# The second half's output projection moved past the scan, on all eight PSUM banks, beside the making of the first MLP operands

## The chip, the cores and the metric

The kernel runs on one core of one Trainium2 chip. The metric is the device time of one execution in microseconds. The kernel before takes 2737.82 us, the median of three runs (2737.07 to 2745.41).

## The reference

One layer of a hybrid decoder on 2048 tokens of width 1024: RWKV-7 time mixing, a delta-rule scan over 12 heads of 64, side by side with a cross-attention into 256 memory tokens. Their outputs are concatenated, projected, and added to the input. A squared-ReLU MLP of width 4096 follows.

```python
h = rms_norm(x, norm_mix_g)
mix, q_mem = rwkv7_time_mix(h, rw_in, ...)          # scan over 2048 tokens
mem_out = memory_cross_attention(q_mem, k_mem, v_mem, ...)
x = x + jnp.concatenate([mix, mem_out], axis=-1) @ w_out
u = rms_norm(x, norm_ffn_g) @ w_ff1
x = x + jnp.square(jax.nn.relu(u)) @ w_ff2
```

## The kernel before, in words

The 2048 tokens are four groups of 512 (`NG`, `G`) or 16 pairs of two 64-token chunks. All large products are done in three passes: each operand is split into a rounded part and a rest (`split`, L92 on ACT, L93 on DVE), and high times high, high times low and low times high are accumulated in PSUM.

There are three stages. In the first, the input projections `project(g)` are made group by group, and `prepare`, `scan` and `post` run over the 16 pairs. `prepare` builds a pair's matrices and solves a small triangular system on DVE, `scan` carries the state, and `post` normalises and writes `mix_d[g]`. In the second, `output(g)` multiplies `mix_d[g]` and `mem_d[g]` by `w_out`, adds `x` and writes `x2_d[g]`. In the third, the MLP runs over two halves of 1024 tokens (`layer1`, `layer2`), each a Strassen-like scheme of seven products in place of eight. Its operands `B` are seven combinations of the normalised, transposed rows of `x2_d`, and `prologue(hf, banks)` makes them.

`output(g)` (L805 to L832) works on quarters of 256 output columns: eight weight tiles are loaded and split for a quarter, then 24 matmuls of 256 columns go into one half bank for each of two row tiles (`rows_mm`, L626). PSUM comes from the pool `psx` of three banks. Group 3 is called in two parts, since its pairs finish one by one; each part loads `w_out` again.

`prologue(0, (3, 4, 6))` loads 128 rows of `x2_d` at a time (L924), squares them on ACT (L926), takes the inverse root on GpSimd (L86), scales on DVE (L928), transposes eight blocks on TensorE (L933), copies to `xraw` on ACT (L936), and then splits and subtracts (L92, L93, L908). Its row buffer `xn` has two copies.

A planner orders the work: every instruction gets a rank (`tc.cur_priority`), lower goes first, and a list scheduler with a timing model turns the ranks into a fixed order for each engine. `dense(first, last, ...)` spreads the steps of a generator over ranks from pair `first` to pair `last`, three pairs behind the scan (`LAG`), 640 ranks to a pair; `CUTS` holds these bounds. So projection work fills the gaps of the scan. After the scan the stage's memory pools are closed, and the pools of the MLP are opened over the same addresses; `reuse_waits` orders new tiles behind the old ones. All loads and stores go through SP's queue. The MLP's PSUM is one pool with eight tags, `b0` to `b7`.

Of the kernel before, what the change touches and what calls it, by code (L numbers as in the profile page):

```python
# [9 lines left out]
F32 = mybir.dt.float32  # L10
F32R = mybir.dt.float32r
# [8 lines left out]
P = 128  # L20
# [29 lines left out]
PAIR_RANKS = 640  # L50
CUTS = [0, 3.17, 8.01, 11.51, 12.67, 13.54, 14.66, 15.27, 15.84]
SPAN = list(zip(CUTS, CUTS[1:]))

# [7 lines left out]
def hybrid_layer(  # L61
# [81 lines left out]
    mem_d = [dram.tile([P, 2, G], F32, name=f"mem_d{g}") for g in range(NG)]  # L143
    mix_d = [dram.tile([P, NB, G], F32, name=f"mix_d{g}") for g in range(NG)]
    x2_d = [dram.tile([G, D], F32, name=f"x2_d{g}") for g in range(NG)]

# [423 lines left out]
    gmc = gain_col(xp, g_mix[0], "gmc")  # L570
    gm = gain_col(xp, g_mem, "gm")
    muc = xp.tile([P, 20], F32, name="muc")
    nc.sync.dma_start(muc, rw_mu[0].rearrange("(b p) -> p b", p=P))
# [231 lines left out]
    def output(g, parts=(0, 1)):  # L805
# [14 lines left out]
        for qq in range(4):  # L820
            csl = slice(qq * 256, (qq + 1) * 256)
            w = weights256(w_out[0][:, csl])
            for t2 in parts:
# [8 lines left out]
                nc.sync.dma_start(x2_d[g][r0 : r0 + 256, csl].rearrange("(t p) c -> p t c", p=P), xr)  # L832


    def memory(*groups):
# [24 lines left out]
    tc.cur_priority = rank["base"] + 20 * PAIR_RANKS  # L860
# [15 lines left out]

    NCH = DFF // 256
    wq = ctx.enter_context(tc.tile_pool(name="c_w", bufs=2, reuse_waits="tile"))
    rp = ctx.enter_context(tc.tile_pool(name="c_r", bufs=16, reuse_waits="tile"))
    tp = ctx.enter_context(tc.tile_pool(name="c_t", bufs=2, reuse_waits="tile"))  # L880
    xs = ctx.enter_context(tc.tile_pool(name="c_x", bufs=1, reuse_waits="tile"))
    sp = ctx.enter_context(tc.tile_pool(name="c_s", bufs=8, reuse_waits="tile"))
    fp = ctx.enter_context(tc.tile_pool(name="c_f", bufs=FBUF, reuse_waits="tile"))
    pso = ctx.enter_context(tc.tile_pool(name="c_ps", bufs=1, space=PSUM, reuse_waits="tile"))

# [3 lines left out]
    def bank(i, shape, name):  # L889
        return pso.tile(shape, F32, tag=f"b{i}", name=name)  # L890

    def ft(name):
        return fp.tile([P, 512], F32, tag="f", name=name)
# [13 lines left out]
    def sub(o, a, b):  # L907
        nc.vector.tensor_tensor(o, a, b, op=ALU.subtract)  # L908
# [3 lines left out]
    def prologue(hf, banks):  # L912

        B = {n: [xs.tile([P, 4, G], F32R, name=f"x{n}{p}") for p in "hl"]
             for n in ("11", "22", "T1", "T3", "T2", "21", "T4")}
        if hf == 0:
            nc.sync.dma_start(gfr, g_ffn.to_broadcast([P, D]))
        nb = 0
        for i in range(4):
            tsl = slice(i * P, (i + 1) * P)  # L920
            raw = {}
            for l in range(2):
# [6 lines left out]
                for j in range(2):  # L929
                    pt = bank(banks[nb % len(banks)], [P, 4, P], "pt")  # L930
                    nb += 1
                    for k in range(4):
                        nc.tensor.transpose(pt[:, k, :], xn[:, (4 * j + k) * P : (4 * j + k + 1) * P], ident)  # L933
                    t = rp.tile([P, 512], F32, tag="r", name="xraw") if hf == 0 else ft("xraw")
# [3 lines left out]
            put = lambda n, src: split(src, B[n][0][:, :, tsl], B[n][1][:, :, tsl])  # L938
            b11, b12, b21, b22 = raw[0, 0], raw[0, 1], raw[1, 0], raw[1, 1]
            put("11", b11)  # L940
            put("22", b22)
            sub(b11, b12, b11)
            put("T1", b11)
            sub(b12, b22, b12)
            put("T3", b12)
            sub(b22, b22, b11)
            put("T2", b22)
            put("21", b21)
            sub(b21, b21, b22)
            put("T4", b21)  # L950
            yield
# [12 lines left out]
    def layer1(hf, B):  # L964
# [127 lines left out]

    tc.cur_priority = rank["base"] + 16 * PAIR_RANKS
    B = list(prologue(0, (3, 4, 6)))[-1]
    tc.cur_priority = rank["base"] + 20 * PAIR_RANKS
    layer1(0, B)
    got = []

    def aside():
# [38 lines left out]
```

## Time and profile before

| | us |
|---|---|
| median of three runs | 2737.82 |
| the profiled execution's own time | 2744.66 |
| its span | 2742.9 |
| TensorE matmul busy | 2610.6 (95%) |
| TensorE weight load busy | 2128.4 (78%) |
| DVE busy | 1811.1 (66%) |
| ACT busy | 1353.9 (49%) |
| GpSimd busy | 235.9 (9%) |
| DMA moved | 519.32 MB, 189 GB/s |

PE is TensorE's matmuls and PEld its weight loads, which overlap; SP is the engine that issues the transfers. Busy time is the union of an engine's instructions, and a matmul counts from its start to its modelled end, so pipelined matmuls overlap and their spacing is less than the mean duration shown. PEclk is the share of full clock that TensorE was granted. A few per cent of the matmul records can be missing, so counts of matmuls are slightly low.

### The profile page before, as it was taken

Reading aid. Unit: us, or ns where it says so; the run is one execution under the profiler, and the core shown is the slowest. Engines: PE = TensorE matmul, PEld = TensorE weight load, DVE = VectorE, ACT = ScalarE, POOL = GpSimd, SP = SyncE. Lnnn points to the kernel's source line nnn. Section 1 sums busy time; section 2 is a strip of 40 time slices with the busy share of each in tenths; the row PEclk is TensorE's granted clock in tenths of the full one; section 3 lists DMA queues with packets and bytes.
Section 4 is the critical chain, followed back from the end, with each engine's and each line's share of the span. In section 5 each row is a group of like instructions: output and inputs, shape, how many; then the busy total and the mean of one; then the engine's idle time right before and its main releaser. Section 6 shows DMA issues by size and latency. Waiting matters only on the chain.

```text
span 2742.9 us, 49338 instructions
## 1 busy us (share of the span) xinstructions
PE 2610.6 (95%) x17620; PEld 2128.4 (78%) x17620; DVE 1811.1 (66%) x4628; ACT 1353.9 (49%) x2925; POOL 235.9 (9%) x172
## 2 busy tenths in 40 slices
PE   6989999999999999979996999999999999999999
PEld 4767777777777777868885888878888888888887
DVE  5556657667767767877558777765866666655564
ACT  5563445445545546553346444444744454544443
POOL 2000011111111111111301000000000000000000
PEclk9999999999999998989997999999999999999999
DMA  8987555556555545355583667886775444456675
GB/s 254 292 265 207 161 172 148 165 151 178 151 155 139 146 134 141 102 140 142 172 257 102 234 232 262 282 304 195 243 260 165 143 150 146 157 193 208 209 255 165
DMA packets 468442, 519.32 MB, mean 189 GB/s; under 512 B 117538, under 2 KB 291682, under 8 KB 468196
## 3 DMA queue, kind: packets, MB, share of 16 engines
q1 hardware_dynamic: 468196, 516.18, 61.0%
q8 instruction: 138, 2.26, 0.3%
q14 instruction: 108, 0.88, 0.1%
HBM read 361.86 MB, written 154.14 MB: 188 GB/s over the span
## 4 chain that ended last, share of the span: by engine, by line
PE 64%; DVE 5%; DMA 4%; ACT 1%; issue 1%; SPq 1%; POOL 0%; DVEq 0%; ACTq 0%; POOLq 0%
PE pu L961 23%; PE py L1070 22%; PE pz L102 5%; PE pout L626 4%; DMA ws<-in_w_out_dram 1%; PE pp L390 1%; DVE zt L428 1%; PE prhs L482 1%; DVE wo L93 1%; PE psco L769 1%; PE pe L463 1%; PE pw L488 1%; PE pe L456 1%; PE pS L495 1%; DVE Zw L432 1%
## 5 line engine op out<-in xcount | busy, mean ns | idle before, releaser
L102 PE MATMUL pz<-xh,w 128*128 128x512 f32 x1408 | 483.0, 412 | 4.3 <-DVE last L678 3.0
L1070 PE MATMUL py<-wpl,hhh 128*128 128x512 f32 x896 | 349.1, 390 | 0.0
L1070 PE MATMUL py<-wph,hhl 128*128 128x512 f32 x896 | 348.4, 389 | 0.0
L1070 PE MATMUL py<-wph,hhh 128*128 128x512 f32 x896 | 343.9, 391 | 0.0
L102 PEld LDWEIGHTS pz<-xh,w 128*128 128x128 f32 x1408 | 267.6, 192 | 71.2 <-issue 6.4
L93 DVE TENSOR_TENSOR hhl<-hr,hhh 128x512 fp32r<-128x512 f32 x224 | 154.6, 690 | 218.4 <-ACT hhh L92 218.0
L92 ACT CAST hhh<-hr 128x512 fp32r<-128x512 f32 x224 | 139.1, 621 | 304.8 <-PE py L1070 281.6
L102 PE MATMUL pz<-xl,w 128*128 128x512 f32 x704 | 287.7, 409 | 0.6 <-DVE xl L93 0.6
L626 PE MATMUL pout<-wo,xh 128*128 128x256 f32 x1024 | 213.6, 302 | 12.9 <-ACT wo L92 7.3
L428 DVE TENSOR_TENSOR zt<-Ti,Zw 96x96 f32<-96x96 f32 (+20 forms) x736 | 154.2, 232 | 72.0 <-DMA Ti<-nd 50.7
L1070 PEld LDWEIGHTS py<-wph,hhl 128*128 128x128 f32 x896 | 168.2, 188 | 34.9
L1070 PEld LDWEIGHTS py<-wph,hhh 128*128 128x128 f32 x896 | 168.2, 188 | 34.6
L1070 PEld LDWEIGHTS py<-wpl,hhh 128*128 128x128 f32 x896 | 168.3, 188 | 34.5
L626 PEld LDWEIGHTS pout<-wo,xh 128*128 128x128 f32 x1024 | 171.9, 202 | 20.3 <-ACT wo L92 8.2
L102 PEld LDWEIGHTS pz<-xl,w 128*128 128x128 f32 x704 | 135.7, 193 | 30.7 <-issue 2.4
L93 DVE TENSOR_TENSOR wpl<-wr,wph 128x512 fp32r<-128x512 f32 x224 | 153.2, 684 | 4.2 <-ACT wph L92 4.2
L432 DVE TENSOR_TENSOR Zw<-Zw,zt 96x96 f32<-96x96 f32 (+20 forms) x736 | 150.3, 227 | 6.5 <-DVE zt L428 0.2
L626 PE MATMUL pout<-wo,xl 128*128 128x256 f32 x512 | 151.9, 297 | 0.2 <-DVE xl L93 0.2
L92 ACT CAST wph<-wr 128x512 fp32r<-128x512 f32 x224 | 138.1, 617 | 9.4 <-PE pu L961 7.0
L390 PE MATMUL pp<-AR,BK 64*128 64x128 f32 x768 | 104.4, 320 | 17.2 <-DVE PT L392 15.0
L390 PEld LDWEIGHTS pp<-AR,BK 64*128 64x128 f32 x768 | 85.6, 214 | 36.3 <-DVE PT L392 18.5
L392 DVE TENSOR_TENSOR PT<-pp,msk 128x384 f32<-128x384 f32 x128 | 67.9, 548 | 62.4 <-PE pp L390 62.1
(292 smaller groups left out, 5496.3 us busy)
## 6 DMA issues: line engine op xcount, KB each, us to landing
w<-w_d SPq DMA_DIRECT2D x264, 256.0 KB, 4.3
hr<-hc_d SPq DMA_DIRECT2D x224, 256.0 KB, 2.8
ws<-in_w_ff_dram SPq DMA_DIRECT2D x32, 1024.0 KB, 5.7
hc_d<-hs SPq DMA_DIRECT2D x128, 256.0 KB, 2.3
wr<-t_d SPq DMA_DIRECT2D x128, 256.0 KB, 3.2
wr<-in_w_ff_dram SPq DMA_DIRECT2D x96, 256.0 KB, 3.1
w_d<-w SPq DMA_DIRECT2D x88, 256.0 KB, 4.3
ws<-in_w_out_dram SPq DMA_DIRECT2D x80, 256.0 KB, 4.4
```

The costliest lines, as they stand in the source:

```text
L92: nc.scalar.copy(hi, src)
L93: nc.vector.tensor_tensor(lo, src, hi.bitcast(F32), op=ALU.subtract)
L102: nc.tensor.matmul(ps, a(k), b(k), start=(k == 0 and i == 0), stop=(k == nk - 1 and i == 2))
L390: nc.tensor.matmul(pps[q][:, j, :], BK[c][rs, b, :], d["AR"][rs, b, :], start=True, stop=True)
L392: nc.vector.tensor_tensor(PT[:, q * NB + 3 * hb : q * NB + 3 * hb + 3, :], pps[q], K["msk"].unsqueeze(1).to_broadcast([P, 3, 2 * C]), op=A ...
L428: nc.vector.tensor_tensor(zt[:, j0:j1, :nt], Ti[:, s, s + 1 :].unsqueeze(1).to_broadcast([96, j1 - j0, nt]), Zw[:, j0:j1, s : s + 1].to_br ...
L432: nc.vector.tensor_tensor(Zw[:, j0:j1, s + 1 :], Zw[:, j0:j1, s + 1 :], zt[:, j0:j1, :nt], op=ALU.add)
L456: nc.tensor.matmul(pe[lo, b, :], d["PT"][:32, q * NB + b, 32:C], te[:, q * NB + b, :], start=True, stop=True)
L463: nc.tensor.matmul(pe[hi, b, :], te2[:, b, :], Z[:, b, lo], start=True, stop=True)
L626: nc.tensor.matmul(po[:, t, :], a(k, t), w[k][:, b], start=(k == 0 and i == 0 and t == 0), stop=(k == KB - 1 and i == 2 and t == 1))
L961: nc.tensor.matmul(ps, a[u][:, k * P : (k + 1) * P], b[v][:, k, :], start=(first and k == 0 and i == 0), stop=(k == 3 and i == 2), skip_gr ...
L1070: nc.tensor.matmul(ps[bk], a[u][:, m * P : (m + 1) * P], b[v], start=(fresh and c == 0 and t == 0), stop=(c == NCH - 1 and t == 2), skip_g ...
```

## The change

Groups 2 and 3 are no longer projected by `output` beside the scan. `late_output` does them after it: the output columns in two halves of 512, eight banks in turn (0 to 3 for the first half, 4 to 7 for the second), four row tiles of 128 for each of the eight k blocks, 192 matmuls of 512 columns for a group. It keeps the split mixer output for both halves, loads `w_out` once for a group, and stores through GpSimd's queue. Between the k steps it advances a generator (`first`), which loads the normalised, transposed rows and makes the seven operands of the first MLP half.

Those rows come from `ffn_rows`, which is put behind `output(1)` in the same call of `dense`. It loads 128 rows of `x2_d`, normalises, transposes into `psx`, applies the gain while copying and writes `xn_d`. The prologue of the second MLP half stays as it was, but for the order of its splits.

The cuts are changed, the operand pool is split in two (`c_x0`, `c_x1`), the pools are opened in another order, and PSUM becomes eight pools of one bank. `layer1` and `layer2` swap banks by half.

```diff
-CUTS = [0, 3.17, 8.01, 11.51, 12.67, 13.54, 14.66, 15.27, 15.84]
+CUTS = [0, 3.17, 8.01, 11.51, 13.9, 15.84]
+    def ffn_rows():
+        for i in range(4):
+            for l in range(2):
+                xt = xrows("xt")
+                nc.sync.dma_start(xt, x2_d[l][i * P : (i + 1) * P, :])
+                rows_norm(xp, xt, xt, xp.tile([P, D], BF16, name="junk"))
+                for j in range(2):
+                    pt = psx.tile([P, 4, P], F32, tag="x", name="pt")
+                    for k in range(4):
+                        nc.tensor.transpose(pt[:, k, :], xt[:, (4 * j + k) * P : (4 * j + k + 1) * P], ident)
+                    rt = small([P, 4, P], "rt")
+                    for k in range(4):
+                        nc.scalar.activation(rt[:, k, :], pt[:, k, :], AF.Copy, scale=gfc[:, 4 * j + k : 4 * j + k + 1])
+                    nc.sync.dma_start(xn_d[i][j, l], rt)
+                    yield
...
-        elif p in (7, 11):
-            dense(*SPAN[p // 4 + 3], (output(p // 4), 64))
-        elif p in (13, 15):
-            dense(*SPAN[p // 2], (output(3, (p // 2 % 2,)), 32))
+        elif p == 7:
+            dense(*SPAN[4], (output(1), 64), (ffn_rows(), 16))
...
-    wq: c_w, rp: c_r, tp: c_t, xs: c_x, sp: c_s, fp: c_f, pso: c_ps (one pool)      [order of opening, in short]
+    xs: c_x0, tp: c_t, rp: c_r, xs2: c_x1, wq: c_w, sp: c_s, fp: c_f, pso: c_ps0 to c_ps7
...
+            for i in range(4):                       # first half: prologue(0, ())
+                raws.append({})
+                for j in range(2):
+                    for l in range(2):
+                        t = rp.tile([P, 512], F32, tag="r", name="xraw")
+                        raws[i][j, l] = t.rearrange("p (k t) -> p k t", k=4)
+                        nc.sync.dma_start(raws[i][j, l], xn_d[i][j, l])
+                yield
+            for n in names:
+                for i in range(4):
+                    combine(i, raws[i], n)
+                    yield
...
-            q = 4 * ((c + 1) % 2)
+            q = 4 * ((c + hf) % 2)
-        X, Y = range(4), range(4, 8)
+        X, Y = (range(4), range(4, 8)) if hf == 0 else (range(4, 8), range(4))
...
-    tc.cur_priority = rank["base"] + 16 * PAIR_RANKS
-    B = list(prologue(0, (3, 4, 6)))[-1]
+    def late_output(beside):
+        for g in (2, 3):
+            ops = []
+            for n in range(2):
+                ps = [bank(4 * n + m, [P, 512], "px") for m in range(4)]
+                csl = slice(n * 512, (n + 1) * 512)
+                for k in range(KB):
+                    if n == 0:
+                        mt = stile("mr")
+                        nc.sync.dma_start(mt, mix_d[g][:, k, :] if k < NB else mem_d[g][:, k - NB, :])
+                        hl = [fp.tile([P, 512], F32R, tag="f", name=f"mx{p}") for p in "hl"]
+                        split(mt, *hl)
+                        ops.append(hl)
+                    if k % 2 == 0:
+                        wt = wq.tile([P, 4, 512], F32R, tag="w", name="wx")
+                    wr = stile("wr")
+                    nc.sync.dma_start(wr, w_out[0][k * P : (k + 1) * P, csl])
+                    b = [wt[:, 2 * (k % 2) + i, :] for i in range(2)]
+                    split(wr, *b)
+                    for m in range(4):
+                        for i, (u, v) in enumerate(((0, 0), (0, 1), (1, 0))):
+                            nc.tensor.matmul(ps[m], ops[k][u][:, m * P : (m + 1) * P], b[v],
+                                             start=(k == 0 and i == 0), stop=(k == KB - 1 and i == 2))
+                    if k % 2 or g == 3 or n:
+                        next(beside, None)
+                for m2 in range(2):
+                    ...                              # xr: load x, add two banks, advance beside
+                    nc.gpsimd.dma_start(x2_d[g][rows, csl].rearrange("(t p) c -> p t c", p=P), xr)
+    tc.cur_priority = rank["base"] + 19 * PAIR_RANKS
+    beside = first()                                 # first() runs prologue(0, ())
+    late_output(beside)
+    for _ in beside:
+        pass
+    tc.cur_priority = max(tc.cur_priority, rank["base"] + 20 * PAIR_RANKS)
+    layer1(0, got[-1])
```

## Rows read from the trace of the kernel before

**Rows 1.** Page, chain that ended last: shares of the span by engine, then by line.

```profile
PE 64%; DVE 5%; DMA 4%; ACT 1%; issue 1%; SPq 1%; POOL 0%; DVEq 0%; ACTq 0%; POOLq 0%
...
PE pu L961 23%; PE py L1070 22%; PE pz L102 5%; PE pout L626 4%; DMA ws<-in_w_out_dram 1%; PE pp L390 1%; DVE zt L428 1%; PE prhs L482 1%; DVE wo L93 1%; PE psco L769 1%; PE pe L463 1%; PE pw L488 1%; PE pe L456 1%; PE pS L495 1%; DVE Zw L432 1%
```

**Rows 2.** By stretch: us; PE, PEld, DVE, ACT, POOL busy (count); PEclk, DMA share, GB/s.

```profile
1064.00:1343.00 279.00, 252.81 (x2891) 223.91 (x2892) 207.85 (x716) 134.03 (x358) 50.13 (x29) 0.91 0.46 128
...
1343.00:1447.00 104.00, 97.28 (x827) 94.60 (x823) 59.03 (x138) 40.57 (x107) 10.58 (x7) 0.97 0.73 231
...
1447.00:1487.00 40.00, 14.44 (x64) 11.20 (x62) 37.41 (x61) 31.66 (x58) 5.83 (x7) 0.57 0.36 112
...
1487.00:1490.00 3.00, 2.42 (x6) 1.96 (x7) 3.00 (x7) 2.51 (x6) 0.46 (x1) 0.50 0.00 0
...
1490.00:1790.00 300.00, 300.00 (x1281) 241.74 (x1280) 224.74 (x357) 140.63 (x242) 2.21 (x1) 0.99 0.71 244
...
1790.00:1798.00 8.00, 5.42 (x24) 4.09 (x23) 4.56 (x7) 5.42 (x10) 0.00 (x0) 0.95 0.95 341
...
2500.00:2740.00 240.00, 239.00 (x1055) 197.59 (x1053) 130.95 (x206) 96.64 (x170) 0.00 (x0) 1.00 0.65 208
```

**Rows 3.** Chain by time, 1310 to 1500 us: start us, us, what.

```profile
1348.49 0.85 PE py L525 x24
...
1429.34 17.43 PE pout L626 x143
...
1448.23 4.33 DMA xn<-x_d
...
1459.84 3.54 DMA xn<-x_d
...
1469.70 3.46 DMA xn<-x_d
...
1487.58 12.48 PE pu L961 x41
```

**Rows 4.** Lines L928, L933, 1330 to 1480: ns min/median/max, first and last start.

```profile
L928 DVE SCALAR_TENSOR_TENSOR xn<-xn,nr,gfr x8: 1276/1282/1286, 1350.5 to 1479.6; 128x1024 f32<-128x1024 f32 x8
...
L933 PE MATMUL pt<-ident,xn x56: 270/421/447, 1446.6 to 1478.4; 128*128 128x128 f32 x56
```

**Rows 5.** Adds by time on DVE; landing of stores L832, 1300 to 1330.

```profile
1313.08 0.69 DVE L831 TENSOR_TENSOR xr<-xr,pout 128x512 f32<-128x512 f32 x1 [1.16 <-PE pout L626]
...
1323.20 0.67 DVE L831 TENSOR_TENSOR xr<-xr,pout 128x512 f32<-128x512 f32 x1
...
DMA to landing us min/median/max: 2.5/2.5/2.5
```

**Rows 6.** Lines L495 and L560, 1300 to 1400: first and last start.

```profile
L495 PE MATMUL pS<-WV,BKT x48: 221/222/270, 1323.4 to 1343.1; 128*64 128x64 f32 x48
...
L560 PE MATMUL pg<-SG,g2s x24: 273/275/422, 1329.3 to 1380.1; 128*128 128x128 f32 x24
```

**Rows 7.** Groups in 2500 to 2740, then L908, L556 and landing of L971.

```profile
L93 DVE TENSOR_TENSOR hhl<-hr,hhh 128x512 fp32r<-128x512 f32 x85 | 58.7, 691 | 100.4 <-ACT hhh L92 100.4
...
L92 ACT CAST hhh<-hr 128x512 fp32r<-128x512 f32 x85 | 52.8, 621 | 134.0 <-PE py L1070 131.2 <-DMA hr<-hc_d 2.8
...
L908 DVE TENSOR_TENSOR xraw<-xraw x16: 677/683/691, 1452.9 to 1493.4; 128x512 f32<-128x512 f32 x16
...
L556 ACT ACTIVATE mixT<-pty,lbc x30: 342/367/377, 1065.9 to 1336.1; 128x128 f32<-128x128 f32 x30
...
DMA to landing us min/median/max: 5.3/7.9/10.5
```

**Rows 8.** DMA in 1343 to 1447: total, and w_out loads with us to landing.

```profile
DMA packets 26069, 24.04 MB, mean 231 GB/s; under 512 B 1376, under 2 KB 25696, under 8 KB 26058
...
ws<-in_w_out_dram SPq DMA_DIRECT2D x40, 256.0 KB, 3.6
```

**Rows 9.** Group in 1343 to 1447: busy, mean ns, idle before and its releasers.

```profile
L92 ACT CAST wo<-ws 128x256 fp32r<-128x256 f32 x87 | 32.0, 404 | 46.9 <-DMA ws<-in_w_out_dram 31.2 <-PE pout L626 14.3 <-DVE wo L93 0.7
```

More of the change, by code (lines that the diff above doesn't have):

```diff
@@ L144, in hybrid_layer @@
     mix_d = [dram.tile([P, NB, G], F32, name=f"mix_d{g}") for g in range(NG)]
+    xn_d = [dram.tile([2, 2, P, 4, P], F32, name=f"xn_d{i}") for i in range(4)]
     x2_d = [dram.tile([G, D], F32, name=f"x2_d{g}") for g in range(NG)]
@@ L571, in hybrid_layer @@
     gm = gain_col(xp, g_mem, "gm")
+    gfc = gain_col(xp, g_ffn[0], "gfc")
     muc = xp.tile([P, 20], F32, name="muc")
@@ L877, in hybrid_layer @@
     NCH = DFF // 256
+    xs = ctx.enter_context(tc.tile_pool(name="c_x0", bufs=1, reuse_waits="tile"))
+    tp = ctx.enter_context(tc.tile_pool(name="c_t", bufs=2, reuse_waits="tile"))
+    rp = ctx.enter_context(tc.tile_pool(name="c_r", bufs=16, reuse_waits="tile"))
+    xs2 = ctx.enter_context(tc.tile_pool(name="c_x1", bufs=1, reuse_waits="tile"))
     wq = ctx.enter_context(tc.tile_pool(name="c_w", bufs=2, reuse_waits="tile"))
-    rp = ctx.enter_context(tc.tile_pool(name="c_r", bufs=16, reuse_waits="tile"))
-    tp = ctx.enter_context(tc.tile_pool(name="c_t", bufs=2, reuse_waits="tile"))
-    xs = ctx.enter_context(tc.tile_pool(name="c_x", bufs=1, reuse_waits="tile"))
     sp = ctx.enter_context(tc.tile_pool(name="c_s", bufs=8, reuse_waits="tile"))
     fp = ctx.enter_context(tc.tile_pool(name="c_f", bufs=FBUF, reuse_waits="tile"))
-    pso = ctx.enter_context(tc.tile_pool(name="c_ps", bufs=1, space=PSUM, reuse_waits="tile"))
+    pso = [ctx.enter_context(tc.tile_pool(name=f"c_ps{i}", bufs=1, space=PSUM, reuse_waits="tile")) for i in range(8)]
     hc_d = [[dram.tile([7, P, G], F32, name=f"hc_d{hf}_{c}") for c in range(NCH)] for hf in range(2)]
@@ L889, in bank @@
     def bank(i, shape, name):
-        return pso.tile(shape, F32, tag=f"b{i}", name=name)
+        return pso[i].tile(shape, F32, tag=f"b{i}", name=name)
     def ft(name):
@@ L912, in prologue, with put, combine @@
     def prologue(hf, banks):
-        B = {n: [xs.tile([P, 4, G], F32R, name=f"x{n}{p}") for p in "hl"]
-             for n in ("11", "22", "T1", "T3", "T2", "21", "T4")}
-        if hf == 0:
-            nc.sync.dma_start(gfr, g_ffn.to_broadcast([P, D]))
+        B = {}
+        def put(i, n, src):
+            if n not in B:
+                B[n] = [(xs2 if n in ("21", "T4") else xs).tile([P, 4, G], F32R, name=f"x{n}{p}") for p in "hl"]
+            split(src, *(t[:, :, i * P : (i + 1) * P] for t in B[n]))
+        def combine(i, raw, n):
+            b11, b12, b21, b22 = raw[0, 0], raw[0, 1], raw[1, 0], raw[1, 1]
+            o, a, b = {"11": (b11, None, None), "22": (b22, None, None), "T1": (b11, b12, b11), "T3": (b12, b22, b12),
+                       "T2": (b22, b22, b11), "21": (b21, None, None), "T4": (b21, b21, b22)}[n]
+            if a is not None:
+                sub(o, a, b)
+            put(i, n, o)
+        names = ("11", "22", "T1", "T3", "T2", "21", "T4")
+        raws = []
+        if hf == 0:
+            for i in range(4):
[10 more added lines that the diff above has]
+                    yield
+            yield B
+            return
+        nc.sync.dma_start(gfr, g_ffn.to_broadcast([P, D]))
         nb = 0
@@ L933, in prologue @@
                         nc.tensor.transpose(pt[:, k, :], xn[:, (4 * j + k) * P : (4 * j + k + 1) * P], ident)
-                    t = rp.tile([P, 512], F32, tag="r", name="xraw") if hf == 0 else ft("xraw")
+                    t = ft("xraw")
                     raw[j, l] = t.rearrange("p (k t) -> p k t", k=4)
@@ L937, in prologue @@
                     yield
[L938 to L950, printed above, removed]
+            for n in names:
+                combine(i, raw, n)
             yield
@@ L1091, in layer2 @@
                     store(0, m, 1, u1[m], q[m])
-    tc.cur_priority = rank["base"] + 16 * PAIR_RANKS
-    B = list(prologue(0, (3, 4, 6)))[-1]
-    tc.cur_priority = rank["base"] + 20 * PAIR_RANKS
-    layer1(0, B)
-    got = []
+    def late_output(beside):
[24 more added lines that the diff above has]
+                for m2 in range(2):
+                    rows = slice(m2 * 256, (m2 + 1) * 256)
+                    xr = tp.tile([P, 2, 512], F32, tag="xn", name="xr")
+                    nc.sync.dma_start(xr, x[g * G + m2 * 256 : g * G + (m2 + 1) * 256, csl].rearrange("(t p) c -> p t c", p=P))
+                    for t in range(2):
+                        add(xr[:, t], xr[:, t], ps[2 * m2 + t])
+                        next(beside, None)
+                    nc.gpsimd.dma_start(x2_d[g][rows, csl].rearrange("(t p) c -> p t c", p=P), xr)
@@ L1099, in aside, with first @@
+    got = []
+    def first():
+        for b in prologue(0, ()):
+            got.append(b)
+            yield
+    tc.cur_priority = rank["base"] + 19 * PAIR_RANKS
[5 more added lines that the diff above has]
+    layer1(0, got[-1])
     def aside():
```

## The prediction

> **What bounds the kernel now.** I read the page's chain of waits first: TensorE holds 64% of it, most in the two MLP layers (L961, L1070), and only 4% belongs to the output projection (L626) [rows 1]. So the kernel is a TensorE kernel, and a change pays where TensorE waits. Second, the table by stretch [rows 2]. From 1490 us on, TensorE is busy all the time at the granted clock 0.99 to 1.00, so nothing in the MLP proper can move. From 1064 to 1343 us (the last third of the scan, with groups 0 and 1 of the projection beside it) TensorE is busy 252.81 of 279.00 us; in-order matmuls of scan and filler share it. From 1343 to 1447 us groups 2 and 3 of the projection run almost alone: 97.28 of 104.00 us busy. From 1447 to 1487 us TensorE is busy 14.44 of 40.00 us at clock 0.57: that is the making of the first MLP operands (prologue), bound by a chain through DMA, ACT, DVE and TensorE, with DVE busy 37.41 us. These last two stretches, 144 us together, are what the change rewrites.
>
> Third, the chain by time [rows 3]: a dense run of the 256-column matmuls takes 17.43 us for 143, 122 ns each; each row block of the prologue costs one round of load, square, scale and transpose, 11.6 and 9.9 us between the load starts at 1448.23, 1459.84 and 1469.70. Fourth, who could have run earlier [rows 4]: the first rows are scaled at 1350.5 us, but the first transpose starts at 1446.6, behind the last projection matmul. The named banks 3, 4 and 6 belonged to scan pools that were long done, so the one pool of eight banks waits for everything that lay in PSUM. I take it that a pool waits for all tiles under its address range; eight pools undo that for PSUM.
>
> **The change part by part.** Times are of the profiled execution, 2744.66 us with a span of 2742.9; it lies 6.8 us above the median 2737.82, and I take differences off that median.
>
> *Columns.* 768 matmuls of 256 columns become 384 of 512. At 122 ns the old ones are 94 us; the new form is that of L1070, 1055 in 239.00 us [rows 2], 226.5 ns, so 87 us. The wider form alone gives 7 us. The Trainium skill (TensorE: Matmul & The Clock Gate, section "Back-to-back issue gap") has 131 ns as the sustained spacing for 512 columns; by it the 384 take 50 us and the result would be some 37 us lower, near 2680. The trace disagrees: 226.5 ns over 1055 matmuls, and the measurement decides.
>
> *Weights.* The old tail loads w_out three times (group 2, and group 3 in two parts), the new one twice. The old stall there is ACT waiting for these loads, 31.2 us [rows 9], of which at most the 6.7 us idle of TensorE are the price [rows 2]. The new tail moves 8.4 MB of weights, 4.2 of mixer output, 4.2 of x, 4.2 of stores, 4.2 of reloaded operands and 1.0 of the first MLP weights, 26 MB; the old one moved 24.04 MB in 104 us [rows 8].
>
> *The prologue leaves the tail.* Its 37 us between the last projection matmul (1446.8) and the steady MLP (1483 to 1488) go [rows 3]. What stays of it is 28 splits and 16 subtractions, now beside the matmuls. DVE in the new tail: 48 projection splits and 28 operand splits at 691 ns, 16 adds and 16 subtractions at 683 ns [rows 7], 74 us; ACT 76 casts at 621 ns, 47 us. Both fit in 87 us, DVE narrowly; if that cover goes, TensorE waits. I charge 6 us of stalls (the old tail had 6.7 us idle in 104 [rows 2]); bounds 0 and 20.
>
> *Row normalisation (ffn_rows) is put behind group 1, beside the scan.* It adds 8 loads of 512 KB, 64 transposes, 64 ACT copies of 128x128 at 367 ns [rows 7] (23 us of ACT, which is half idle there [rows 2]) and 16 stores. Its transposes use the three banks of the scan's projection pool, and the late projection's banks 0 to 2 lie under them; its operand pools lie under the pools of ffn_rows and of group 1 too. So the late projection cannot start before the last transpose of ffn_rows. That is what is late next. Before, group 1 ends with the add at 1323.20 (the rows of its first half at 1313.08), and a store lands 2.5 us later [rows 5]. So blocks 0 and 1 may start at 1317, all at 1327. Four rounds at 10 us [rows 3] end at 1357 to 1367; I take 1362. The scan's last state matmul is at 1343.1 and its last post-processing at 1380.1 [rows 6]; without group 2 in its way the latter comes earlier, and the late projection asks for it only in its second half.
>
> *Start of the late projection.* A 256 KB load lands in 3.6 us [rows 8], then a cast 0.62 and a subtraction 0.69 us [rows 7], with semaphores 6 us: first matmul 1368. TensorE has then been idle and starts at the granted clock 0.50, as the MLP does now (1487 to 1490 us [rows 2]; 41 matmuls in 12.48 us [rows 3], some 3 us lost). The lost time moves with the gap, so it cancels.
>
> *Start of the MLP.* The first weight tile shares two buffers with the late weights and can be loaded only when two of the last k remain: 24 matmuls, 5.4 us, against a landing of 5.3 to 10.5 us [rows 7] and a split. I charge 5 us; bounds 2 and 8. The banks are free, since the last projection half uses 4 to 7 and the MLP begins on 0 to 3.
>
> *Priorities, GpSimd stores, the bank swap of the second layer.* Nothing: TensorE shows no gap at those places now. The new cuts give group 1 a lower priority than before; as it is filler already, I charge nothing and keep a slide of up to 37 us as a rival.
>
> **Sum.** 1362 + 6 + 87 + 6 + 5 = 1466, and the steady MLP begins at 1487 today: 21 us less, 2737.8 - 21 = 2717 us. With each small term at its ends (ffn_rows 1357 to 1367, stalls 0 to 20, MLP start 2 to 8) the forecast's own range is 2702 to 2739.
>
> **Rivals.**
> *A, ffn_rows fully hidden.* If group 1 ends some 20 us earlier, only the scan's own end at 1349 [rows 3] gates: 1349 + 6 + 87 + 2 = 1444, 43 us less, 2695. For it: the scan is no longer slowed by group 2's weight splits. Against it: TensorE is 91% busy from 1064 to 1343 [rows 2], so the same filler can hardly end earlier.
>
> *B, the tail becomes a DMA tail.* 26 MB at the old tail's 231 GB/s [rows 2] take 113 us instead of 87 + 6: 20 us more, 2737, no change; the bytes move and nothing is won. For it: DMA share 0.73 at 231 GB/s, most transfers 256 KB. Against: 341 GB/s stood for 8 us at share 0.95 [rows 2], and the layer-2 loop takes 512 KB for 12 matmuls with TensorE never idle. The Trainium skill (DMA: Bandwidth & Descriptors, section "Bandwidth") wants 1 MiB per transfer for three quarters of peak, which speaks for B; no run here yet shows this tail.
>
> *C, slower: group 1 slides behind the scan.* The place is the last scan pair. If the scheduler lets all scan work go first, group 1's adds end near 1360 instead of 1323; ffn_rows then runs alone, and each microsecond of the slide costs one: 37 - 21 = 16 us more than before, 2754. It decides from a slide of 29 us (21 plus the 8 that count as no change). For it: the rank of group 1 drops by 1.2 to 1.9 pairs. Against it: group 0 and 1 ran as filler at a time later than their cuts, so rank was not what held them.
>
> *D, the change doesn't do what it says:* the eight bank pools or the reordered operand pools still wait for all of the scan. The late projection would then begin after the last post-processing; at 1380.1 as now, that is 1380 + 6 + 87 + 6 + 5 = 1484, 3 us less, 2735: no change.
>
> **Chances.** Forecast 0.46, A 0.18, B and D together 0.18, C and other ways to lose (stalls on DVE at their upper bound on top of a late start) 0.18. About 0.3%, 8 us, is what a measurement of this kernel can tell from no change. The forecast's own case is faster except for its upper tail of about 0.02: faster 0.62, same 0.20, slower 0.18. The range takes A whole and goes into C until a tenth is left out above: 2694 to 2748; the likeliest case alone is 2702 to 2739.
>
> **What would show it.** In the changed profile: the last transpose of ffn_rows near 1362 (step right if within 10 us), the first late matmul 4 to 8 us after it, 384 late matmuls in 87 to 95 us with TensorE at 95% or more, DVE at some 80% there, the first MLP matmul within 8 us of the last late one and no idle 40 us stretch. Wrong, if late matmuls are spaced over 260 ns (B, or DVE), if ffn_rows ends before the scan (A), or if group 1's last add comes after 1345 (C).

## The result, and the profile after

The changed kernel takes 2709.32 us (median of 4 runs, 2701.33 to 2712.15) against 2737.45 us (4 runs, 2730.49 to 2745.41) of the kernel before: ratio 0.9892, 95% interval 0.9856 to 0.9927, faster by 28 us. The forecast was 2717. The profiled execution of after took 2706.92 us (span 2705.2), 2.4 us below its median; that of before lay 7.2 us above this median. So the two profiles differ by 37.7 us, of which some 10 belong to the two executions picked.

The table by stretch of after, to be held against [rows 2]: us; PE, PEld, DVE, ACT, POOL busy (count); PEclk, DMA share, GB/s.

```profile
1064.00:1304.00 240.00, 222.18 (x2438) 196.68 (x2438) 189.09 (x666) 115.62 (x312) 38.21 (x25) 0.93 0.44 124
1304.00:1349.00 45.00, 30.05 (x413) 25.30 (x414) 16.34 (x47) 34.19 (x103) 13.89 (x12) 0.81 0.60 175
1349.00:1356.00 7.00, 4.93 (x142) 4.45 (x140) 2.18 (x9) 4.14 (x13) 0.00 (x0) 1.00 0.92 286
1356.00:1465.00 109.00, 96.34 (x402) 76.23 (x402) 72.12 (x121) 43.55 (x82) 14.77 (x12) 0.95 0.68 233
1465.00:1468.00 3.00, 1.73 (x7) 1.08 (x7) 2.86 (x5) 0.62 (x1) 0.58 (x1) 1.00 0.40 100
1490.00:1790.00 300.00, 299.45 (x1304) 244.13 (x1303) 225.59 (x361) 143.86 (x252) 0.00 (x0) 1.00 0.77 268
```

The stretches are the scan with groups 0 and 1 beside it, the row normalisation (ffn_rows), the start of the late projection, the late projection, the MLP's start, and layer 1. The reader is to see three things. The idle 40 us stretch at clock 0.57 is gone; a smaller one, 1304 to 1349 us with 30.05 of 45.00 us busy at clock 0.81, is new. The MLP starts at clock 1.00 and no longer at 0.50. And 300 us of layer 1 now hold 1304 matmuls where [rows 2] had 1281, with TensorE as busy as before: the matmuls themselves come faster. The transposes of ffn_rows and the two forms of the late matmul, each with ns min/median/max, first and last start:

```profile
L846 PE MATMUL pt<-ident,xt x64: 272/273/476, 1304.5 to 1348.7; 128*128 128x128 f32 x64
...
L1154 PE MATMUL px<-wx,mxh x256: 387/389/797, 1356.4 to 1464.5; 128*128 128x512 f32 x128
L1154 PE MATMUL px<-wx,mxl x128: 387/389/632, 1357.7 to 1464.7; 128*128 128x512 f32 x128
```

The chain by time of after (start us, us, what), which answers to [rows 3]: a late load of the mixer output, a late weight load, the densest run of late matmuls, and layer 1.

```profile
1354.67 4.97 DMA mr<-mix_d
...
1365.40 5.17 DMA wr<-in_w_out_dram
...
1426.00 33.65 PE px L1154 x140
...
1467.09 52.97 PE pu L999 x230
```

Cut at the first matmul of the output projection and the first of the MLP, the two profiles give this (us; the scatter is that of part 1 over 14 profiles, 1052 to 1068, most of them with the same order of work there):

| | start to first pout | first pout to first pu | first pu to end |
|---|---|---|---|
| before | 1064.9 | 419.9 | 1258.1 |
| after | 1061.9 | 403.9 | 1239.4 |

Between these two profiles, 16 us come from the tail that the change rewrites, where 21 were forecast, and 18.7 us from the MLP, of which the prediction said that nothing in it can move. The tail of before is a long one: in the other three profiles with the old pools and the old projection (e1, e9 and e12 below) the middle column is 414.1, 418.9 and 413.1 us, so the tail's gain is 9 to 16 us. The last column of e9 and e12, whose MLP is that of before, is 1257.2 and 1258.9 us, so the MLP's gain holds. The experiments go after both.

### The profile page after: what moved, and what is told of

Its sections match the earlier page's. It is cut to its first block, busy times and chain, and to the rows that moved or that the text cites. A ratio compares the mean times of both kernels' runs of the same rounds, so it can differ in the third digit from the quotient of the medians.

```text
span 2705.2 us, 48412 instructions
## 1 busy us (share of the span) xinstructions
PE 2578.1 (95%) x17236; PEld 2093.3 (77%) x17236; DVE 1800.2 (67%) x4564; ACT 1344.5 (50%) x2909; POOL 233.9 (9%) x180
## 4 chain that ended last, share of the span: by engine, by line
PE 75%; DMA 9%; DVE 7%; ACT 4%; issue 2%; SPq 2%; POOL 1%; DVEq 0%; ACTq 0%; POOLq 0%
PE py L1108 22%; PE pu L999 18%; PE pz L102 14%; PE pout L628 3%; PE pp L391 2%; PE px L1154 2%; DMA ws<-in_w_ff_dram 1%; PE py L520 1%; DVE zt L429 1%; DVE Zw L433 1%; PE py L526 1%; PE prhs L483 1%; PE pw L489 1%; PE pe L464 1%; PE pe L457 1%
## 5 line engine op out<-in xcount | busy, mean ns | idle before, releaser
L429 DVE TENSOR_TENSOR zt<-Ti,Zw 96x96 f32<-96x96 f32 (+20 forms) x736 | 161.3, 242 | 51.7 <-DMA Ti<-nd 36.9
L433 DVE TENSOR_TENSOR Zw<-Zw,zt 96x96 f32<-96x96 f32 (+20 forms) x736 | 158.2, 237 | 6.4
L628 PE MATMUL pout<-wo,xh 128*128 128x256 f32 x512 | 111.5, 307 | 7.6 <-ACT wo L92 6.6
L391 PE MATMUL pp<-AR,BK 64*128 64x128 f32 x768 | 94.7, 317 | 21.1 <-DVE PT L393 19.2
L391 PEld LDWEIGHTS pp<-AR,BK 64*128 64x128 f32 x768 | 78.4, 211 | 38.4 <-DVE PT L393 23.2
L628 PEld LDWEIGHTS pout<-wo,xh 128*128 128x128 f32 x512 | 87.4, 203 | 13.2 <-ACT wo L92 7.7
L1154 PE MATMUL px<-wx,mxh 128*128 128x512 f32 x256 | 84.2, 407 | 13.0 <-DVE wx L93 9.5
```

The costliest lines, as they stand in the source:

```text
L391: nc.tensor.matmul(pps[q][:, j, :], BK[c][rs, b, :], d["AR"][rs, b, :], start=True, stop=True)
L429: nc.vector.tensor_tensor(zt[:, j0:j1, :nt], Ti[:, s, s + 1 :].unsqueeze(1).to_broadcast([96, j1 - j0, nt]), Zw[:, j0:j1, s : s + 1].to_br ...
L433: nc.vector.tensor_tensor(Zw[:, j0:j1, s + 1 :], Zw[:, j0:j1, s + 1 :], zt[:, j0:j1, :nt], op=ALU.add)
L628: nc.tensor.matmul(po[:, t, :], a(k, t), w[k][:, b], start=(k == 0 and i == 0 and t == 0), stop=(k == KB - 1 and i == 2 and t == 1))
L1154: nc.tensor.matmul(ps[m], ops[k][u][:, m * P : (m + 1) * P], b[v], start=(k == 0 and i == 0), stop=(k == KB - 1 and i == 2))
```

## The experiments

Theories. *Addresses*: the MLP's matmuls are faster because the operand tiles lie elsewhere in SBUF; in the compiled programs the moving and the stationary operand of layer 1 lie at byte offsets 128 and 192 modulo 256 in before, at 192 and 128 (1920 matmuls) or at 128 and 128 (768) in after. In layer 2 the two offsets are equal in both kernels: 192 and 192 in before, 128 and 128 in after. *Pools*: the tail is shorter because the first MLP operands no longer wait for the whole of PSUM and SBUF. *Late projection*: it is shorter by the wide matmuls with the operands made beside them. *Banks*: the MLP gains because layer 1 of the first half no longer ends on the four banks that layer 2 takes next.

**e1_pad_before**: before, with 64 bytes more in one tile that lies below the operand tiles; the order of every engine stays the same.

```diff
-tp.tile([P, D], BF16, name="junk", bufs=1)
+tp.tile([P, D + 32], BF16, name="junk", bufs=1)[:, :D]
```

> The kernel before with one tile of its row pool c_t widened by 64 bytes, so that the operand tiles of layer1 shift by 64 bytes against the weight tiles; every engine's order stays. Addresses theory: matmuls of layer1 are spaced 233 ns before because moving and stationary operand lie at different offsets modulo 128 bytes (0 and 64), and 226.7 ns in layer2 where both lie at 64; with the pad both lie at 64, so layer1's spacing falls to 226 to 228 ns, 2688 x 6.6 ns = 18 us less, 2720 us. Rival: the spacing in layer1 comes from the order of products or from twelve matmuls in a row into one bank; then nothing moves, 2737 us.

Measured 2720.72 us, ratio 0.9946 (0.9929 to 0.9963). Here are matmuls of layer 1's second half in 220 us in which TensorE never idles (columns as above without POOL, of the instructions on the tile pu alone), for before, after and e1:

```profile
2160.00:2380.00 220.00, 220.00 (x944) 176.40 (x943) 38.36 (x56) 12.89 (x22) 1.00 0.43 148
```

```profile
2160.00:2380.00 220.00, 220.00 (x963) 180.35 (x962) 39.09 (x57) 13.52 (x23) 1.00 0.45 154
```

```profile
2160.00:2380.00 220.00, 220.00 (x973) 182.26 (x972) 39.64 (x58) 13.45 (x23) 1.00 0.45 156
```

220 us over 944, 963 and 973 matmuls: 233, 228 and 226 ns (mean between starts 233.3, 229.0, 226.7). With all at the same offset, 192, layer 1 runs at layer 2's 226.7. 64 bytes alone are worth 15 us of 2737. That the spacing in layer 1 follows where the tiles lie is shown: the addresses are all that the edit changes.

**e2_pad_after**: the same 64 bytes in after.

> The changed kernel with the same 64 bytes. Addresses theory: there 1920 of layer1's 2688 matmuls have operands at 64 and 0 modulo 128 (spaced 229 ns, some 231) and 768 at 0 and 0; the pad brings all to 64 and 64, so some 2.4 ns x 2688 = 6 us less, 2703 us, and no layer1 product above 228 ns. Rival: nothing moves, 2709 us.

Measured 2701.87 us, 0.9881 (0.9861 to 0.9900); spacing 226.7. The time is where it was expected, but the interval overlaps that of after (0.9856 to 0.9927), so the last 2 ns are not told apart from nothing.

**e3_pools_before**: before with after's order of the operand pools and its eight PSUM pools; no ffn_rows, no late projection, banks as before.

```diff
-wq = ... "c_w" ... (with rp "c_r" ahead of tp "c_t")
+xs = ... "c_x0" ...
 tp = ... "c_t" ...
-xs = ... "c_x" ...
+rp = ... "c_r" ...
+xs2 = ... "c_x1" ...
+wq = ... "c_w" ...
-B = {n: [xs.tile([P, 4, G], F32R, name=f"x{n}{p}") for p in "hl"]
+B = {n: [(xs2 if n in ("21", "T4") else xs).tile([P, 4, G], F32R, name=f"x{n}{p}") for p in "hl"]
-pso = ctx.enter_context(tc.tile_pool(name="c_ps", bufs=1, space=PSUM, reuse_waits="tile"))
+pso = [ctx.enter_context(tc.tile_pool(name=f"c_ps{i}", bufs=1, space=PSUM, reuse_waits="tile")) for i in range(8)]
-return pso.tile(shape, F32, tag=f"b{i}", name=name)
+return pso[i].tile(shape, F32, tag=f"b{i}", name=name)
```

> The kernel before with the changed kernel's pools alone: operand pool in two, pools opened in its order, eight pools of one PSUM bank; prologue, projection and cuts as before. Pools theory: the first half's operands need only groups 0 and 1, and what kept the prologue behind the projection of groups 2 and 3 were the pools; its transposes then start near 1353 instead of 1446 us, most of the 40 us stretch with an idle TensorE goes, and layer1's spacing falls to 229 to 231 ns as well: 2737 - 25 to 40 = 2697 to 2712 us, as fast as the whole change. Rival (late projection theory): the prologue's rows and the projection share ACT, DVE and the queue, and the gain comes from the late projection and ffn_rows; then only the spacing pays, 8 to 12 us, 2725 to 2729 us.

Measured 2709.47 us, 0.9904 (0.9886 to 0.9922): as fast as the whole change. First pout to first pu takes 404.1 us, after's 403.9. The transposes of the first MLP operands in e3, to be held against [rows 4]:

```profile
L934 PE MATMUL pt<-ident,xn x64: 270/273/447, 1352.3 to 1405.1; 128*128 128x128 f32 x64
```

They start at 1352.3 instead of 1446.6, inside the second half's projection: half 0 of the MLP needs only groups 0 and 1, so nothing but the pools held its operands back. The pools theory is shown; beside it the late projection adds nothing that can be measured in the time. e3 also has the new addresses (layer 1 at 229 ns; first pu to end 10.9 us shorter than in before). It keeps the old bank order, and its MLP still starts at clock 0.50.

**e4_serial_after**: after, with the making of the operands behind the late projection in program order.

```diff
-late_output(beside)
+late_output(iter(()))
```

> The changed kernel with the operands of the first half made after the late projection, not beside it. Overlap theory: DVE's 28 splits and 16 subtractions (30 us) and the 16 loads stand alone again; the late projection loses its stalls of 20 us (1356 to 1465 us becomes some 90 us), and 30 to 35 us come behind it: 10 to 20 us more than the change, 2719 to 2729 us. Rival: the stalls of the late projection are not of the operands' making (weight loads, the last post-processing); then it stays at 105 us and 30 to 35 us are added, 2740 to 2745 us.

Measured 2693.95 us, 0.9853 (0.9820 to 0.9886). Both expectations fell: it is not slower. The edit does less than its name: the scheduler fills the operand work in beside the projection anyway, only at a lower rank. The late stretch, and 20 us of it:

```profile
1344.00:1447.00 103.00, 94.90 (x402) 76.49 (x402) 71.40 (x121) 43.74 (x83) 14.74 (x12) 0.95 0.70 245
1380.00:1400.00 20.00, 15.19 (x56) 11.67 (x55) 20.00 (x34) 14.12 (x27) 0.00 (x0) 0.83 0.59 190
```

71.40 us of DVE work stand in 103 us, as in after. In the 20 us DVE is busy all the time, and TensorE 15.19 us. Against after (0.9892) the intervals overlap, so that it is faster is not shown either.

**e6_banks_after**: after with the bank order of before.

```diff
-q = 4 * ((c + hf) % 2)
+q = 4 * ((c + 1) % 2)
-X, Y = (range(4), range(4, 8)) if hf == 0 else (range(4, 8), range(4))
+X, Y = range(4), range(4, 8)
```

> The changed kernel with the bank order of layer1 and layer2 as before in both halves. Bank theory: before, the first half's layer1 ends on banks 0 to 3, which layer2 takes next, and TensorE stops for 2.6 us at 1797.8 and then runs at the granted clock 0.50 for a while; in the changed kernel both are gone. Undone, the stop comes back near the end of the first layer1, and besides the first product waits for banks 4 to 7 of the last late half: 5 to 9 us between the first layer1 matmul and the end, the stretch goes from 1239 back to some 1246 us. Rival: the stop came from ACT's backlog in that execution and not from the banks; then the stretch stays at 1238 to 1241 us.

Measured 2712.77 us, 0.9932 (0.9911 to 0.9954). TensorE by time (start us, us, instruction, idle before and its releaser), first before, then e6:

```profile
1797.79 0.80 PE L961 MATMUL pu<-x21h,a12h 128*128 128x512 f32 x1 [2.58 <-ACT u L994]
1798.38 0.63 PE L961 MATMUL pu<-x21l,a12h 128*128 128x512 f32 x1
```

```profile
1766.89 0.80 PE L999 MATMUL pu<-x21h,a12h 128*128 128x512 f32 x1 [2.58 <-ACT u L1032]
1767.49 0.63 PE L999 MATMUL pu<-x21l,a12h 128*128 128x512 f32 x1
```

The stop of 2.58 us and the slow matmuls behind it come back; after has neither. In after, 52 matmuls of layer 2 start ahead of the last one of layer 1's first half, in before and e6 only 6: with other banks free, layer 2 fills the wait. First pu to end is 1243.8 us in e6 and 1239.4 in after: 4.4 us, just under the 5 to 9 expected. The stop is shown to be the bank order's; the whole time does not tell e6 from after (0.9892), their intervals overlap.

**e9_pz_before**: before, with 32 bytes in the input projection's junk tiles, which puts its stationary operand from 224 to 0 modulo 256, the moving one staying at 128.

```diff
-rows_norm(xp, xt, xt, xp.tile([P, D], BF16, name="junk"))
+rows_norm(xp, xt, xt, xp.tile([P, D + 16], BF16, name="junk")[:, :D])
```

> The kernel before with one tile of the projection's pool a_x widened by 32 bytes, so that the weights of the input projection move from 96 to 0 modulo 128 bytes, as its other operand, and those of the output projection from 96 to 0 too; every engine's order stays. Addresses theory: the 2112 matmuls of the input projection fall from 234 to 227 ns. In the first stage TensorE is busy nearly all the time, so up to 2112 x 7 = 15 us go, and 8 to 15 us are expected: 2722 to 2728 us. The two operands then differ by 128 modulo 256; if the rule goes modulo 256, nothing moves. Rival: the scan's own chain sets the time of that stage; then the spacing falls and the time stays, 2736 us.

Measured 2728.87 us (10 runs), 0.9980 (0.9961 to 0.9999). In a dense run of 209 matmuls from 75 us on the spacing goes from 234.3 to 232.4 ns: equal offsets modulo 128 are not enough.

**e10_late_best**: after with the edits of e4, 64 bytes (e2) and 32 bytes (e9).

> The changed kernel with the operands' order behind the late projection, the 64 bytes in c_t and 32 bytes in a_x (both operands at 32 modulo 128 in the projection). If the gains add up: 2694 - 7 - (8 to 15) = 2672 to 2679 us. If the 9 us by which the order's run began the projection of group 0 earlier were chance: up to 2688 us.

Measured 2694.76 us, 0.9862 (0.9841 to 0.9882). The single gains do not add up.

**e11_early_best**: e3 with after's bank order, 64 bytes and 32 bytes; still no late projection.

> The kernel before with the changed kernel's pools and its bank order, and the 64 and 32 bytes, but with the projection of groups 2 and 3 as before, without ffn_rows and without the late projection. Theory that the pools and addresses carry the gain: 2709 - 6 (the rest of layer1's spacing) - 5 (bank order) - 8 to 15 (input projection) = 2683 to 2690 us, within 10 us of the late version. Rival, that the late projection is worth its 16 us or more once the addresses are right: 2695 us or more.

Measured 2701.63 us, 0.9884 (0.9866 to 0.9902), slower than expected. It overlaps after and e10, and it is level with e2 (2701.87), which has the late projection, the same bank order and the 64 bytes (the 32 bytes are e11's alone). Its first pout to first pu took 403.7 us, e10's 393.6.

**e12_pz256_before**: as e9 with 160 bytes (`D + 80`), so that both operands of the input projection lie at 128 modulo 256.

> As the run with 32 bytes, but 160: the two operands of the input projection now lie at the same offset modulo 256 bytes (128 and 128), and those of the output projection too; every engine's order stays as before. With 32 bytes (equal modulo 128, 128 apart modulo 256) the spacing only went from 233.9 to 232.4 ns. Addresses theory, modulo 256: it falls to 226 to 228 ns, and 2112 x 7 = 15 us of TensorE's time go, of which the scan's chain may give back some: 2718 to 2728 us. Rival, modulo 128 or a rule of other pools only: 232 ns and 2729 to 2734 us.

Measured 2730.55 us (10 runs), 0.9979 (0.9964 to 0.9994). The same dense run of TensorE by time, first before, then e12:

```profile
80.26 0.39 PE L102 MATMUL pz<-xl,w 128*128 128x512 f32 x1
...
80.96 0.40 PE L102 MATMUL pz<-xl,w 128*128 128x512 f32 x1
```

```profile
80.88 0.39 PE L102 MATMUL pz<-xl,w 128*128 128x512 f32 x1
...
81.56 0.39 PE L102 MATMUL pz<-xl,w 128*128 128x512 f32 x1
```

Three matmuls take 0.70 us in before and 0.68 in e12; over the dense run it is 234.3 and 226.8 ns. So in this loop the short spacing comes with offsets that are equal modulo 256. But 2112 such matmuls at 7 ns would be 15 us, and only 6 show in the median, no more than in e9 (5). Part of the answer is that over all gaps between neighbouring matmuls of the projection the mean falls only from 234.1 to 229.2 ns, some 10 us in all. That the scan's own chain takes the rest back is argued and not shown.

**e13_late_256**: e10 with 160 in place of 32 bytes.

> The late version with the operands' order behind the projection and the 64 bytes, now with 160 bytes in a_x (both operands of the input projection at 160 modulo 256). Addresses theory: spacing 227 instead of 232.4 ns, 5 to 11 us less than with 32 bytes: 2684 to 2690 us. Rival, the scan's chain sets the time of that stage: 2694 us.

Measured 2700.66 us, 0.9867 (0.9834 to 0.9900): no gain over e10; the rival's 2694 lies in its interval, 2684 to 2690 do not. Its spacing did fall (median 227.5 ns), so the matmuls came faster and the time did not follow. Its first pout to first pu took 403.2 us with the same order of the late projection as e10, so e10's 393.6 are not that order's doing alone.

**e5_256_after**: after, with each late matmul as two of 256 columns.

```diff
-nc.tensor.matmul(ps[m], ops[k][u][...], b[v], ...)
+for c2 in range(2):
+    nc.tensor.matmul(ps[m][:, c2 * 256 : (c2 + 1) * 256], ops[k][u][...], b[v][:, c2 * 256 : (c2 + 1) * 256], ...)
```

> The changed kernel with each late matmul of 512 columns as two of 256, everything else the same. Prediction's step: 768 at 122 ns take 94 us and 384 at 226.5 take 87, so 7 us more at most, and less if the late projection waits for DVE and loads anyway: 2709 to 2716 us. Rival, the 512 columns are what the change lives by: 2725 us or more.

Measured 2709.24 us, 0.9906 (0.9878 to 0.9934): after's time. The late projection in e5 by stretch:

```profile
1358.00:1467.00 109.00, 98.75 (x786) 97.50 (x786) 72.10 (x122) 44.29 (x83) 14.51 (x12) 0.97 0.68 234
```

768 narrow matmuls fill the same 109 us that 384 wide ones fill in after; TensorE is busy 98.75 instead of 96.34 us, out of the stalls. So the 512 columns are worth nothing that the time shows here.

**e8_psum_before**: before with the eight PSUM pools alone.

> The kernel before with PSUM as eight pools of one bank and nothing else. Pools theory: a pool waits for all that lay under its address range; then the prologue's first transposes start near 1353 us instead of 1446, but the split operands still wait, since the one operand pool lies over the buffers of the output projection, so the four row blocks' raw copies are made early and the 28 splits and 16 subtractions (30 us of DVE) stay behind the projection: 8 to 15 us less, 2720 to 2727 us. Rival: the transposes waited for their rank and not for the pool; then nothing moves, 2734 us.

Measured 2732.49 us (10 runs, 2720.74 to 2745.51), 0.9986 (0.9965 to 1.0008), unclear. The mechanism is there; the same transposes in e8:

```profile
L933 PE MATMUL pt<-ident,xn x64: 270/272/421, 1335.5 to 1406.0; 128*128 128x128 f32 x64
```

In its profile the tail is as short as in e3 (405.0 us), yet the median moved by no clear amount. The profile is at the fast end of its runs. e3, with the operand pools and the new addresses too, is clearly faster. How much of a median the shorter tail is worth by itself therefore stays open: 11 us of e3's 26 are addresses, which leaves some 15, and e8 shows 4 (10 at most by its interval). Two things narrow the gap: the old tails took 413.1 to 419.9 us, so that 405.0 is 8 to 15 us less; and e8's first pu to end is 1261.6 us, some 3 more than in before, for a reason that stays open.

## Why the prediction was right, and where it failed

*The sum of the tail* came out right, 1467.09 against 1466, but by terms that cancel, and 3 us of it is only that the output projection began earlier in this execution (first pout 1061.9, not 1064.9).

- **ffn_rows**: the last transpose is at 1348.7, not 1362, and outside my 10 us. I took group 1's end from [rows 5], but without group 2 beside it, and with the new cuts, it ended early enough for transposes at 1304.5; which of the two did it, no run separates. The four rounds took 44 us, where 40 were forecast.
- **Start of the late projection**: 7.7 us behind the last transpose, 6 forecast. But the last transpose is not all that gated it (rows below).
- **Columns**: the median spacing is 227 ns, as in [rows 2]. The 7 us that the wide form saves vanish in the stalls (e5). The Trainium skill (TensorE: Matmul & The Clock Gate, section "Back-to-back issue gap") has 131 ns; the trace disagrees here too.
- **Stalls**: this is the mis-sized term of the tail. 384 matmuls lasted 1356.4 to 1464.7, 108 us where 87 and 6 were forecast, so 21 us of stalls, just over my upper bound of 20. TensorE is busy 96.34 of 109 us (88%, not 95), and the mean spacing is 282 ns, over the 260 that the prediction named as a sign of being wrong.
- **Start of the MLP**: 1 to 2 us instead of 5, and the half-clock restart of [rows 3] (41 matmuls in 12.48 us) is gone with the gap that caused it; I had said that it would move and cancel.

*A term put at nothing: what ffn_rows does to the scan.* The prediction charged ffn_rows 23 us of ACT, "which is half idle there", and nothing to the scan. Here are the chain of after by time, its last state matmuls (for [rows 6], which has 1343.1), and a stretch of before to hold against the 30.05 us above:

```profile
1333.05 1.61 PE pt L846 x8
...
1335.15 0.87 PE pS L496 x24
1336.05 2.18 ACT rt L849 x8
...
1348.84 1.83 ACT rt L849 x7
...
1351.39 0.85 PE py L526 x21
```

```profile
L496 PE MATMUL pS<-WV,BKT x72: 222/222/270, 1307.9 to 1352.8; 128*64 128x64 f32 x72
```

```profile
1304.00:1349.00 45.00, 40.08 (x525) 36.75 (x525) 20.56 (x49) 19.02 (x46) 10.68 (x6) 0.92 0.61 178
```

The chain goes in turn through the copies of ffn_rows (rt), its transposes (pt) and the scan (pS, py). Counted from the first pout, the last state matmul starts at 278 us in before and 291 in after; over all profiles it is 272 to 281 us in the seven without ffn_rows and 286 to 295 in the seven with it. The first load of w_out is issued at 1352, released by the scan's last py matmuls, and ffn_rows issues its last store at 1351.04: both ends gate the late projection, and in these two profiles the scan's has moved back by some 13 us. TensorE meanwhile is busy 30.05 us of 45 where before, with group 2's matmuls as filler, it is busy 40.08. So the change pays for its shorter tail with a slower end of the scan and with stalls, which fits that e3, with neither ffn_rows nor a late projection, is as fast. No run takes ffn_rows alone out of after, so how much of the 13 us is its doing stays open.

What the stalls are, by stretches of 10 us of the late projection in after (columns as above, with POOL):

```profile
1356.00:1366.00 10.00, 7.85 (x32) 5.84 (x33) 6.15 (x20) 4.14 (x8) 0.55 (x1) 1.00 0.98 347
1366.00:1376.00 10.00, 8.14 (x34) 5.78 (x32) 6.84 (x5) 3.70 (x6) 9.52 (x5) 1.00 1.02 376
...
1396.00:1406.00 10.00, 8.89 (x28) 7.09 (x29) 10.00 (x17) 7.47 (x14) 0.00 (x0) 0.67 0.44 136
1406.00:1416.00 10.00, 9.12 (x40) 7.03 (x39) 10.00 (x18) 4.37 (x9) 0.00 (x0) 1.00 0.41 126
1416.00:1426.00 10.00, 7.04 (x32) 5.48 (x30) 10.00 (x18) 5.91 (x11) 1.46 (x2) 1.00 0.58 191
1426.00:1436.00 10.00, 10.00 (x37) 8.13 (x38) 4.85 (x8) 1.14 (x2) 0.00 (x0) 0.83 0.96 336
1436.00:1446.00 10.00, 10.00 (x46) 8.29 (x45) 5.29 (x8) 2.28 (x4) 1.45 (x2) 1.00 0.25 88
```

and the longest stops of TensorE in it, by time:

```profile
1356.44 1.43 PE L1154 MATMUL px<-wx,mxh 128*128 128x512 f32 x5 [1.74 <-ACT wx L92]
1361.18 1.69 PE L1154 MATMUL px<-wx,mxh 128*128 128x512 f32 x5 [1.71 <-ACT wx L92]
...
1397.11 0.80 PE L1154 MATMUL px<-wx,mxh 128*128 128x512 f32 x1 [3.40 <-DVE wx L93]
...
1426.00 0.50 PE L1154 MATMUL px<-wx,mxh 128*128 128x512 f32 x1 [2.96 <-DVE wx L93]
```

At first the DMA engines are full (share 0.98 to 1.02) and casts and splits come as the loads do: rival B, for the first 30 us or so only. Then DVE is full from 1396 to 1426, where the operand work is pressed together, and TensorE waits for its weight splits, 3.40 and 2.96 us at a time; after each of these stops the granted clock is low (0.67 and 0.83). From 1436 on, with DVE half idle, TensorE is busy all the time. Idle time is 13 us of the 109, the lower clock costs an estimated 3.3 and 1.7 us by these shares, and the scan's last 18 matmuls take some of the rest. The sum of DVE's work was right, 72.12 us for 74, but a sum that fits into a stretch is not one that fits at every moment.

*The step that failed* is "nothing in the MLP proper can move", with "the bank swap: nothing". A TensorE that is busy all the time can still take fewer ns for each matmul, and the profile of before showed both signs. Layer 1 and layer 2 have the same form, yet [rows 2] give 300.00/1281 = 234 ns and 239.00/1055 = 226.5 ns. I read both rows and used only the second. And in the row 1790 to 1798 TensorE is busy 5.42 of 8.00 us, so there was a gap where the prediction says that there is none. In the place of these steps the runs showed three things. The 2688 matmuls of layer 1 come 4.3 ns closer, 11 us (e1: the spacing follows the addresses; e3, which of the three has this alone, is 10.9 us shorter from the first pu to the end). The stop of 2.58 us at 1797.79 goes with the bank order (e6: 4.4 us). The restart at half clock is gone, an estimated 3 us: 41 matmuls in 12.48 us in [rows 3], against 52.97/230 = 230 ns each, 9.4 us for 41, in after. Together 18 to 19 of the 18.7 us.

*Rival A* was right on its condition, group 1 ended 18.5 us earlier (last add 1304.7 for 1323.20), and wrong in the total: it left the scan's end at 1349 and had no stalls. *Rival D* was wrong in the right place: the new pools do let go, and that is where the tail's gain comes from, with or without a late projection. *Rival C* did not occur.

The direction was right, and the mechanism in part: the idle stretch before the MLP did go, but the pools remove it, and the late projection, the wide matmuls and ffn_rows add nothing that was measured. That 2709 came out near 2717 is in good part luck: the tail gave 9 to 16 us where 21 were forecast, and the MLP gave 18.7 where none were.

The best version measured is the late one with the operands behind it: 0.9853 (e4), 0.9862 (e10, with the pads) and 0.9867 (e13). All beat before; against after (0.9892) the intervals overlap.

## What to carry to other kernels

Before a phase boundary is rewritten, open one pool for each bank and each lifetime, and see when the next phase's first instruction could have run: here the pools, with the new addresses that came with them, gave what the whole rewrite gave. Where two loops have the same matmul and one of them is 3% slower without any idle time, look at where the operand tiles lie, and change one tile's size before changing anything else. A filler that fits by its sum must be laid out over time on the engine that it fills, against every other burst on it. And work that is put beside a chain, as ffn_rows beside the end of the scan, must be charged to that chain, even on an engine that is half idle.

## What the runs showed of the hardware

- In these runs the spacing of 512-column matmuls goes with the byte offsets of the two operands modulo 256, as read from the compiled programs: 226.7 to 226.9 ns where they are equal (192/192 in e1 and in layer 2 of before, 128/128 in layer 2 of after and in the dense run of e12), 229 to 234 ns where they differ (moving/stationary 192/128 229, 128/0 232.4, 128/192 233, 128/224 234). It is not the whole rule: one tile of after at 128/128 (x21) stayed near 231 ns, while another (xT4) has 227; why stays open.
- Behind the stop of 2.58 us of TensorE (e6; before has the same one) the granted clock is 0.50, 1.2 GHz of 2.4, where it was 1.00 in the 9 us ahead of it (1755 to 1764). The matmuls behind the stop start 0.43 us apart instead of 0.23. The first 2 us behind it in e6, by stretch:

```profile
1766.90:1769.00 2.10, 2.10 (x5) 1.72 (x6) 2.07 (x5) 0.00 (x0) 0.00 (x0) 0.50 0.85 304
```

- A split on DVE takes 0.69 us, and 1.9 to 2.3 us while GpSimd runs element-wise work on SBUF. DVE, then POOL of after by time:

```profile
1369.33 0.69 DVE L93 TENSOR_TENSOR mxl<-mr,mxh 128x512 fp32r<-128x512 f32 x1 [1.40 <-ACT mxh L92]
1370.00 1.91 DVE L93 TENSOR_TENSOR wx<-wr,wx 128x512 fp32r<-128x512 f32 x1
1371.83 2.32 DVE L93 TENSOR_TENSOR mxl<-mr,mxh 128x512 fp32r<-128x512 f32 x1
1374.07 2.31 DVE L93 TENSOR_TENSOR wx<-wr,wx 128x512 fp32r<-128x512 f32 x1
1376.31 0.68 DVE L93 TENSOR_TENSOR mxl<-mr,mxh 128x512 fp32r<-128x512 f32 x1
```

```profile
1369.37 1.99 POOL L542 TENSOR_TENSOR yc<-yc,mean 128x768 f32<-128x768 f32 x1
1371.44 2.17 POOL L543 TENSOR_TENSOR yc<-yc,lgr 128x768 f32<-128x768 f32 x1
1373.68 2.15 POOL L546 TENSOR_TENSOR yc<-yc,Vn 128x768 f32<-128x768 f32 x1
```

The three slow splits cost 4.5 us more than three of 0.69, and the splits are fast again once GpSimd is done (1375.8). The Trainium skill (SBUF — State Buffer, section "Who interferes with whom") says that a DVE instruction with two inputs in SBUF contends with a GpSimd instruction that reads SBUF; the trace agrees, 0.69 against 2.3 us.
